# A planned opening: x split from PSUM, sums on GpSimd, and a planner that repeats its plan

## The chip, the cores and the metric

The kernel runs on one core of a Trainium2 chip. Its time is the device time of one execution in microseconds (us). TensorE is called PE here (PEld is its weight load), VectorE DVE, ScalarE ACT, GpSimd POOL and SyncE SP, as in the profile.

## The reference

One layer of a gated decoder trunk over 1024 prompt tokens and 8 sample tokens, width 1024, all in float32. What matters here:

```python
xn = _rmsnorm(h, pre_g)
proj = jnp.einsum('bld,de->ble', xn, w_in)
u, v, z_a, x_b, z_b, g_a, g_b = jnp.split(proj, SPLITS, axis=-1)
...
m = (jax.nn.sigmoid(g_a) * jnp.einsum('ble,ed->bld', y_a, w_pa)
     + jax.nn.sigmoid(g_b) * jnp.einsum('ble,ed->bld', y_b, w_pb))
h = h + _rmsnorm(jnp.einsum('bld,de->ble', m, w_out), post_g)
e = jnp.einsum('blp,pd->bld', p, w_ple)
gate = jax.nn.sigmoid(jnp.einsum('bld,de->ble', _rmsnorm(h, ple_in_g), w_pg))
h = h + _rmsnorm(gate * e, ple_out_g)
```

`y_a` and `y_b` come from two branches (a causal mix within chunks of 128 tokens, and a causal pooling), which the change does not touch. The outputs are the new h of both kinds of token and four state buffers.

## The kernel before

**Products.** Every float32 matrix is split into two parts that PE can multiply fast: `hi`, the value rounded to fp32r, and `lo`, what is left (`split`: ACT copies to hi, DVE subtracts). A product is three matmuls, hi x hi, hi x lo and lo x hi, added up in PSUM. The large products (seven column blocks of W_in, then W_pa, W_pb, W_out, W_pg) are made in 2 x 2 blocks by Strassen's scheme with seven block products, P1 to P7; the first pair of columns of v is made in the plain way with eight, as its right-hand sides are the first to be there. The right-hand sides of the scheme are four blocks of the activation (B11, B12, B21, B22: feature half, token half) and four combinations of them (T1 to T4), which `combine` makes in place in the tile `big` and `cut` splits. `product` issues the 12 matmuls of a block product, for four k, as one unit of the plan.

**The opening** (`begin`). p, W_ple, x and the first weights are loaded. 24 transposes of the identity keep PE going until data is there (`warm`). The embedding e = p W_ple is made for token tiles of 128: `p_turn` transposes and splits p, `embed` makes 2 x 6 matmuls into a PSUM region, `embed_out` copies the region to SBUF on ACT and stores it for the end of the kernel. For each x tile, ACT makes a sum of squares (`norm_root`), DVE adds epsilon, GpSimd raises to the power -0.5, and DVE scales the tile (`norm_scale`). `x_half(j, kps)` then transposes token half j of x, 8 transposes for each pair of feature blocks kp, and evacuates them with the gain from PSUM into `big`, on DVE for even kp and on ACT for odd. `xop.cut` reads `big` again to split a block: 1024 elements a partition on ACT, then on DVE. Until the end of `begin` the order of every engine is the one written there (`plan.fixed = True`).

**The planner.** Nothing is issued as it is written. `Planner.take` records each call with its duration by a formula (`duration`: for DVE 0.065 + 0.00105 us an element, plus 0.06 for scalar_tensor_tensor; for GpSimd 1.0 us for all but memset), and finds from the memory that a call touches what must come before it. Consecutive PE calls into one PSUM tile are one op, unless `apart` is called between them. `wanted` gives each op a time by which it is due (`late`), backwards from the PE ops that need it. `order` then plays the program: at each step it takes, of the ops that could start soonest, the one that is due first, and keeps a clock for each engine, for the DMA pipe and for the 46 slots of SBUF that tiles share. The order in which ops start there is the order in which the engines get their instructions; each engine works through its own in that order. PSUM is shared by 3 regions of two banks (`region`: e, pst, acc, acct) and 2 single banks (`bank`).

**The end.** The last large product is the gate h' W_pg. Its right-hand sides are pieces of W_pg (loaded as wgB and wgT, split to wgB11h, wgB11l and so on), its left-hand sides are turned tiles of the normalised h (`hn`, transposed as `pht`, split as `hw`). W_pg's pieces are loaded and split while the product before it (`acct<-woB..`) runs. h itself is put together by a DMA that adds x in flight, and then stored (`h<-h` on SP).

All instructions that pass through the planner show line 289 in the profile (`play`), so they are told apart by their tiles. [Tile names: `ph`, `pl` are the parts of p; `wehi`, `welo` of W_ple; `vw` of a weight block of v; `xB11h` and so on of x.]

Of the kernel before, what the change touches and what calls it, by code (L numbers as in the profile page):

```python
# [14 lines left out]
P = 128  # L15
D = 1024
NB = D // P
# [37 lines left out]
class Planner:  # L55
# [116 lines left out]
    def wanted(self):  # L172

        for tag, most in self.queues.items():
            live = []
            for name in [n for n in self.users if self.tags.get(n) == tag]:
                first = next(iter(self.users[name]))
                if len(live) == most:
                    over = [(max(o.seq for o in self.users[n]), n) for n in live]
                    old = min(x for x in over if x[0] < first.seq)[1]  # L180
                    first.before.update(self.users[old])
                    live.remove(old)
                live.append(name)
        for op in self.ops:
            op.waits = len(op.before)
            op.fresh = {n for n in op.names if self.tags.get(n) == "slot"}
            for o in op.before:
                o.after.append(op)
        for op in reversed(self.ops):
            took = op.busy + (op.lands + op.moved / self.RATE if op.moved else self.SEEN.get(op.engine, 0))  # L190
            ends = [o.late - took for o in op.after] + ([op.at] if op.engine == "tensor" else [])
            op.late = min(ends, default=min(op.at + 30.0, self.clock + 12.0))

    def order(self):


        self.wanted()
        free = dict.fromkeys(self.ENGINES, 0.0)
        ready = {e: [] for e in self.ENGINES}
        fixed = {e: [o for o in self.ops if o.engine == e and o.fixed][::-1] for e in self.ENGINES}  # L200
# [95 lines left out]
def hybrid_step(  # L296
# [520 lines left out]

    def x_half(j, kps):

        for kp in kps:  # L820
            ps = region("pst")
            for kk in range(2):
                k = 2 * kp + kk
                for i in range(4):
                    nc.tensor.transpose(ps[:, kk, i * P : (i + 1) * P],
                                        xts[4 * j + i][:, k * P : (k + 1) * P], ident)
# [692 lines left out]
    def p_turn(h):  # L1519
        hi, lo = pcut[h] = slot("ph", (P, 2, HALF), F32R), slot("pl", (P, 2, HALF), F32R)  # L1520
        for k in range(2):
# [4 lines left out]
            if h == 0:  # L1526
                we.cut(k)
# [20 lines left out]


    def begin():  # L1550
        psl = slot("psamp", (P, PLE))
        p_load(0)
        we.fetch(0, nc.scalar)
        for i, v in enumerate((pre_g, pool_scale, ple_in_g)):
            dma(vecs[i * NB : (i + 1) * NB, :], v[0].rearrange("(k p) -> k p", p=P), nc.scalar)
        we.fetch(1)
        for t in range(4):
            x_load(t)
        dma(xe[:NS], x_sample)
# [18 lines left out]
        norm_root(0)  # L1578
        norm_root(1)
        norm_scale(0)  # L1580
        embed(1)
        norm_root(2)
        norm_scale(1)
        norm_root(3)
        norm_scale(2)
        norm_root(S)
        norm_scale(3)
        vps = bank("vecs")
        nc.tensor.transpose(vps[:, : 3 * NB], vecs[: 3 * NB, :], ident[: 3 * NB, : 3 * NB])
        nc.vector.tensor_copy(gvec, vps[:, : 3 * NB])  # L1590
        norm_scale(S)
        embed_out(0)
        x_half(0, (0,))
        embed_out(1)
        norm_root(4)
        x_half(0, (1,))
        x_extra()
        x_half(0, (2,))
        norm_root(5)
        norm_scale(4)  # L1600
        x_half(0, (3,))
        embed(2)
        xop.cut("B11")
        norm_scale(5)
        steps[0].prepare()
        embed(3)
        xop.cut("B21")
        steps[0].run()
        norm_root(6)
        norm_root(7)  # L1610
        norm_scale(6)
        embed_out(2)
        embed_out(3)
        norm_scale(7)
# [26 lines left out]

    gvec = cpool.tile([P, 3 * NB], F32, tag="gvec", name="gvec")
    begin()
    plan.fixed = False
    for s in range(3):
        for f in steps[s].after:
            f()
# [33 lines left out]
```

## Time and profile before

| | us |
|---|---|
| median of 3 runs | 1006.89 (1005.75 to 1007.22) |
| the profiled execution | 1006.03 |
| its span, first to last instruction | 1003.7 |
| PE busy | 987.7 (98%) |
| DVE busy | 798.0 (80%) |
| ACT busy | 488.1 (49%) |
| POOL busy | 78.1 (8%) |

The granted clock of PE was 0.998 of full speed. The span is what the trace covers; 2.3 us of the execution lie around it. A row of the waits names the engine and the tile that waited, what it waited for, the us in total, how many times and the longest. A row of the order of time has the start, the duration, the engine, the line, the operation, its output and inputs, shapes and count, and in brackets the idle time before it with what ended it. An instruction's duration is longer than its pitch, since the next one of the same engine starts before it has drained.

### The profile page before, as it was taken

The numbers are of one execution on the slowest core, as the hardware profiler recorded it, in microseconds if no ns is written. First come the engines' busy times: TensorE is split into PE (matmuls) and PEld (weight loads), VectorE is DVE, ScalarE is ACT, GpSimd is POOL, SyncE is SP. The second block draws the span as 40 slices with busy tenths as digits, with TensorE's granted clock in tenths as the row PEclk, the third lists the DMA queues.
The fourth block names the chain that finished last, engine by engine and source line by source line (L and its number), as shares of the span: only waits on it lengthen the run. The fifth ranks groups of instructions, "written<-read, shape, count | busy, mean of one in ns | idle before, by whom it ended". The sixth has DMA issues, their size and how long they took to land. (4 is left out here: it accounts for less than half of the span.)

```text
span 1003.7 us, 16146 instructions
## 1 busy us (share of the span) xinstructions
PE 987.7 (98%) x6200; PEld 887.4 (88%) x6200; DVE 798.0 (80%) x1237; ACT 488.1 (49%) x887; POOL 78.1 (8%) x162
## 2 busy tenths in 40 slices
PE   8999999999999999999999999999999999998996
PEld 6889999999999999999999999999999988887885
DVE  5985448977689898887776987697799898779796
ACT  7664356555434334232433333562353365678563
POOL 2200001000000000000010100000000002312121
PEclk9999999999999999999999999999999999999999
DMA  9231213222364675441304176973764543397437
GB/s 355 115 119 43 84 43 129 85 85 86 128 234 184 233 273 197 170 169 54 120 18 146 38 249 216 313 284 122 244 222 152 181 153 84 88 305 260 128 77 219
DMA packets 85089, 160.65 MB, mean 160 GB/s; under 512 B 7422, under 2 KB 47406, under 8 KB 85005
## 3 DMA queue, kind: packets, MB, share of 16 engines
q1 hardware_dynamic: 82645, 151.72, 43.3%
q0 software_dynamic: 2048, 7.37, 4.3%
q8 instruction: 48, 0.79, 0.3%
q10 hardware_dynamic: 320, 0.54, 0.2%
q14 instruction: 28, 0.23, 0.1%
HBM read 112.49 MB, written 47.58 MB: 159 GB/s over the span
## 5 line engine op out<-in xcount | busy, mean ns | idle before, releaser
L289 DVE TENSOR_TENSOR u<-acc,u 128x520 f32<-128x520 f32 (+1 forms) x90 | 62.5, 695 | 38.7 <-PE acc L289 34.0
L289 POOL TENSOR_TENSOR rstd<-ms,mhalf 128x1 f32<-128x1 f32 (+1 forms) x45 | 41.6, 927 | 213.8 <-DVE ms L289 191.5
L289 POOL MEMSET u<- 128x8 f32 x35 | 3.5, 105 | 548.8 <-PE acc L289 268.8
L289 ACT ACTIVATE u<-acc 128x512 f32<-128x512 f32 x39 | 23.2, 595 | 36.2 <-PE acc L289 35.9
L289 ACT ACTIVATE paw<-pas 128x512 fp32r<-128x512 f32 x16 | 10.1, 629 | 30.8 <-DVE pas L289 25.5
L289 ACT ACTIVATE pbw<-pbs 128x512 fp32r<-128x512 f32 x16 | 10.0, 628 | 28.7 <-DVE pbs L289 25.5
L289 DVE TENSOR_TENSOR big<-big 128x1024 f32<-128x1024 f32 (+4 forms) x20 | 23.6, 1216 | 0.0
L289 ACT ACTIVATE zbw<-zbs 128x512 fp32r<-128x512 f32 x16 | 9.9, 628 | 27.9 <-DVE zbs L289 24.5
L289 DVE TENSOR_TENSOR xb<-acc,u 128x520 f32<-128x520 f32 (+1 forms) x12 | 8.3, 694 | 19.1 <-PE acc L289 19.1
L289 ACT ACTIVATE big<-vt 128x256 f32<-128x256 f32 x32 | 11.9, 380 | 21.4 <-PE vt L289 21.4
L289 ACT ACTIVATE big<-pht,gvec 128x128 f32<-128x128 f32 x64 | 18.0, 398 | 7.5 <-PE pht L289 7.5
L289 PE MATMUL accm<-qh,wpoolw 128*128 128x260 f32 (+1 forms) x96 | 20.9, 319 | 0.0
L289 ACT ACTIVATE big<-mix 128x256 f32<-128x256 f32 x32 | 12.1, 383 | 17.5 <-PE mix L289 16.9
L289 ACT ACT_TABLE_LOAD x13 | 16.7, 1283 | 2.9 <-PE acc L289 1.6
L289 DVE TENSOR_TENSOR v<-acc,u 128x520 f32<-128x520 f32 (+1 forms) x9 | 6.3, 697 | 14.9 <-PE acc L289 14.8
L289 DVE TENSOR_TENSOR acc<-acc,u 128x512 f32<-128x512 f32 (+1 forms) x16 | 11.1, 696 | 8.7 <-PE acc L289 8.7
L289 ACT ACTIVATE gbw<-gbs 128x512 fp32r<-128x512 f32 x16 | 10.0, 624 | 16.3 <-DVE gbs L289 14.4
L289 PEld LDWEIGHTS accm<-qh,wpoolw 128*128 128x128 f32 x96 | 15.6, 188 | 1.9
L289 DVE SCALAR_TENSOR_TENSOR zb<-accm,gvec,zb 128x512 f32<-128x512 f32 (+1 forms) x16 | 12.0, 751 | 6.6 <-PE accm L289 6.5
L289 ACT ACTIVATE xbw<-xbs 128x512 fp32r<-128x512 f32 x16 | 9.8, 624 | 14.7 <-DVE xbs L289 12.2
L289 DVE TENSOR_TENSOR big<-mix,big 128x256 f32<-128x256 f32 x32 | 13.1, 420 | 4.4 <-ACT big L289 3.5
L289 ACT ACTIVATE uw<-us 128x512 fp32r<-128x512 f32 x16 | 9.8, 627 | 13.8 <-DVE us L289 5.2
(689 smaller groups left out, 3618.3 us busy)
## 6 DMA issues: line engine op xcount, KB each, us to landing
ga<-ga SPq DMA_DIRECT2D x16, 516.0 KB
gb<-gb SPq DMA_DIRECT2D x16, 516.0 KB
ya<-za SPq DMA_DIRECT2D x8, 516.0 KB
yb<-zb SPq DMA_DIRECT2D x8, 516.0 KB
x<-in_x_prompt_dram SPq DMA_DIRECT2D x8, 512.0 KB
vraw<-in_w_in_dram SPq DMA_DIRECT2D x8, 512.0 KB
e<-e SPq DMA_DIRECT2D x8, 512.0 KB
garaw<-in_w_in_dram SPq DMA_DIRECT2D x8, 512.0 KB
```

Of the source, the lines that this page charges most:

```text
L289: getattr(getattr(self.nc, e), method)(*args, **kwargs)
```

## The change

- *Opening.* `plan.fixed` ends after the loads, so the warm-up, the embedding, the norms, x and the first products are planned like the rest. All of W_ple is loaded from SP's queue, behind the first p; before, one half went by ACT's queue. Embeddings 0 to 3 come ahead of x in program order (which also is the order in which PSUM regions are handed on), and x's halves ahead of the sample's.
- *W_ple* is split in pieces of 512 columns (`we_cut`). `embed` makes the four matmuls with W_ple's high part first, and then the two with its low part, as two units of the plan. The e copies of tiles 0 to 3 move from ACT to DVE.
- *x.* `x_half` makes hi (ACT, with the gain) and lo (DVE, scalar_tensor_tensor: PSUM times gain minus hi) straight from PSUM, 512 columns at a time. GpSimd adds hi and lo into `big`, which now serves the combinations alone. `xop.cut` of B11, B21, B12 and B22 is gone; the 8 sample columns of the second half are split from `big` as before.
- *Planner.* A GpSimd operation is priced at 0.1 + 0.0015 us an element, at least 1.0. All users of a reused buffer, not the first alone, wait for the users of the old one. `product` becomes two units, k = 0, 1 and k = 2, 3. The plan is made 40 times (`once`): after each, `hurry` looks for gaps of over 0.2 us between PE ops, goes back from the op behind the gap, up to 8 steps, each time to what ended last before it, and makes each of these due earlier. The due times that gave the earliest modelled end are used for the final plan.

```diff
@@ Planner
-    SPARED = 1.0
+    SPARED, PASSES, DEPTH = 1.0, 40, 8
...
-        return 0.1 + n * 0.0008 if method == "memset" else 1.0
+        return 0.1 + n * 0.0008 if method == "memset" else max(1.0, 0.1 + n * 0.0015)
...
-                    first.before.update(self.users[old])
+                    for user in self.users[name]:
+                        user.before.update(self.users[old])
...
     def order(self):
         self.wanted()
+        tries = []
+        for n in range(self.PASSES):
+            late = [o.late for o in self.ops]
+            self.once()
+            tries.append((max(o.end for o in self.ops), n, late))
+            self.hurry()
+        for o, o.late in zip(self.ops, min(tries)[2]):
+            pass
+        return self.once()
+
+    def hurry(self):
+        last = 0.0
+        for o in sorted((o for o in self.ops if o.engine == "tensor"), key=lambda o: o.start):
+            gap, last = o.start - last, o.end
+            for _ in range(self.DEPTH if gap > 0.2 else 0):
+                if not o.before:
+                    break
+                o = max(o.before, key=lambda b: (b.end, b.seq))
+                o.late -= min(gap, 1.0) + 0.3
@@ product
         for k in range(4):
+            if k == 2:
+                plan.apart()
@@ x_half
         for kp in kps:
-            ps = region("pst")
+            two = region("pst") if kp < 3 else None
+            ps = [bank("pst") if two is None else two[:, kk] for kk in range(2)]
...
-            out = quarter(kp, j)[:, :, :HALF]
+            hi, lo = xop.new(f"B{kp // 2 + 1}{j + 1}", kp % 2)
             for kk in range(2):
-                o, i, gain = out[:, kk], ps[:, kk], col(0, 2 * kp + kk)
-                if kp % 2:
-                    nc.scalar.activation(out=o, in_=i, func=AF.Copy, scale=gain)
-                else:
-                    nc.vector.tensor_scalar_mul(o, i, gain)
+                h, i, gain = hi[:, kk, :HALF], ps[kk], col(0, 2 * kp + kk)
+                nc.scalar.activation(out=h, in_=i, func=AF.Copy, scale=gain)
+                nc.vector.scalar_tensor_tensor(out=lo[:, kk, :HALF], in0=i, scalar=gain, in1=f32(h),
+                                               op0=ALU.mult, op1=ALU.subtract)
+            nc.gpsimd.tensor_tensor(out=quarter(kp, j)[:, :, :HALF], in0=f32(hi[:, :, :HALF]),
+                                    in1=f32(lo[:, :, :HALF]), op=ALU.add)
+            if j:
+                split(quarter(kp, j)[:, :, HALF:], hi[:, :, HALF:], lo[:, :, HALF:])
@@ we_cut, in place of we.cut(k) in p_turn
+        for k in range(2):
+            split(raw[:, k], hi[:, k], lo[:, k])
@@ embed
-            token_matmul([(ps[:, n], lambda k: hi[:, k, tok], lambda k: lo[:, k, tok])], we, n)
+            plan.apart()
+            terms = [(part[:, k, tok], we.at(n, k)[0]) for k in range(2) for part in (hi, lo)]
+            terms += [(hi[:, k, tok], we.at(n, k)[1]) for k in range(2)]
+            for i, (p, w) in enumerate(terms):
+                if i == 4:
+                    plan.apart()
+                nc.tensor.matmul(ps[:, n], p, w, start=i == 0, stop=i == 5)
@@ embed_out
-        nc.scalar.activation(out=e, in_=e_ps.pop(t), func=AF.Copy)
+        if t < 4:
+            nc.vector.tensor_copy(e, ps)
+        else:
+            nc.scalar.activation(out=e, in_=ps, func=AF.Copy)
@@ begin
-        we.fetch(0, nc.scalar)
+        we.fetch(0)
+        we.fetch(1)
...
         early_loads()
+        plan.fixed = False
...
         p_turn(0)
+        we_cut(0)
+        we_cut(1)
+        for t in range(4):
+            norm_root(t)
+            norm_scale(t)
         embed(0)
...
+        x_half(0, (0, 1))
+        steps[0].prepare()
+        x_half(0, (2, 3))
...
         steps[0].evacuate()
         x_half(1, (0, 1))
+        steps[1].run()
         p_turn(1)
         x_half(1, (2, 3))
-        steps[1].run()
-        xop.cut("B12")
         embed(4)
-        xop.cut("B22")
```

More of the change, by code (lines that the diff above doesn't have):

```diff
@@ L184, in wanted @@
         for op in self.ops:
-            op.waits = len(op.before)
-            op.fresh = {n for n in op.names if self.tags.get(n) == "slot"}
             for o in op.before:
@@ L197, in order, with once @@
         self.wanted()
+        tries = []
[16 more added lines that the diff above has]
+                o.late -= min(gap, 1.0) + 0.3
+    def once(self):
+        for o in self.ops:
+            o.waits, o.ready = len(o.before), 0.0
+            o.fresh = {n for n in o.names if self.tags.get(n) == "slot"}
         free = dict.fromkeys(self.ENGINES, 0.0)
@@ L824, in x_half @@
                 for i in range(4):
[L825 removed]
+                    nc.tensor.transpose(ps[kk][:, i * P : (i + 1) * P],
                                         xts[4 * j + i][:, k * P : (k + 1) * P], ident)
[L827 removed]
+            hi, lo = xop.new(f"B{kp // 2 + 1}{j + 1}", kp % 2)
             for kk in range(2):
[L829 to L833 removed]
+                h, i, gain = hi[:, kk, :HALF], ps[kk], col(0, 2 * kp + kk)
[6 more added lines that the diff above has]
+                split(quarter(kp, j)[:, :, HALF:], hi[:, :, HALF:], lo[:, :, HALF:])
     def x_extra():
@@ L1525, in p_turn, with we_cut @@
             split(ps, hi[:, k], lo[:, k])
-            if h == 0:
-                we.cut(k)
+    def we_cut(n):
+        raw = we.raw.pop((n, 0))
+        hi, lo = slot("wehi", (P, 2, HALF), F32R), slot("welo", (P, 2, HALF), F32R)
+        for k in range(2):
+            split(raw[:, k], hi[:, k], lo[:, k])
+        we.hi[n, 0], we.lo[n, 0] = hi, lo
     e_ps = {}
@@ L1535, in embed @@
         for n in range(2):
-            token_matmul([(ps[:, n], lambda k: hi[:, k, tok], lambda k: lo[:, k, tok])], we, n)
+            plan.apart()
[5 more added lines that the diff above has]
+                nc.tensor.matmul(ps[:, n], p, w, start=i == 0, stop=i == 5)
     def embed_out(t):
         e = slot("e", (P, 2, HALF))
-        nc.scalar.activation(out=e, in_=e_ps.pop(t), func=AF.Copy)
+        ps = e_ps.pop(t)
+        if t < 4:
+            nc.vector.tensor_copy(e, ps)
+        else:
+            nc.scalar.activation(out=e, in_=ps, func=AF.Copy)
         dma(kept["e"][t * P : (t + 1) * P].rearrange("p (n c) -> p n c", n=2), e)
@@ L1576, in begin @@
         p_turn(0)
+        we_cut(0)
[3 more added lines that the diff above has]
+            norm_scale(t)
         embed(0)
-        norm_root(0)
-        norm_root(1)
-        norm_scale(0)
+        embed_out(0)
         embed(1)
[L1582 to L1587, printed above, removed]
+        embed_out(1)
+        embed(2)
+        embed_out(2)
+        embed(3)
+        embed_out(3)
         vps = bank("vecs")
@@ L1590, in begin @@
         nc.vector.tensor_copy(gvec, vps[:, : 3 * NB])
+        x_half(0, (0, 1))
+        steps[0].prepare()
+        x_half(0, (2, 3))
+        norm_root(S)
         norm_scale(S)
[L1592 to L1596, printed above, removed]
-        x_extra()
[L1598 to L1614, printed above, removed]
+        steps[0].run()
+        x_extra()
+        for t in range(4, NB):
+            norm_root(t)
+            norm_scale(t)
         steps[1].prepare()
@@ L1643, in hybrid_step @@
     begin()
-    plan.fixed = False
     for s in range(3):
```

1 line of the change is left out of this document (removed).

## The prediction

> **What bounds the kernel now.** First the head of the page and the engines' shares, then the list of what TensorE (PE) waited for.
>
> ```profile
> span 1003.7 us, 16146 instructions
> ...
> PE 987.7 (98%) x6200; PEld 887.4 (88%) x6200; DVE 798.0 (80%) x1237; ACT 488.1 (49%) x887; POOL 78.1 (8%) x162
> ```
>
> ```profile
> PE warm L289 <- POOL ident masks.py:199: 1.9, 1, 1.9
> PE acct L289 <- DVE ms L289: 1.6, 1, 1.6
> PE acct L289 <- DVE hw L289: 1.2, 1, 1.2
> PE e L289 <- ACT wehi L289: 1.2, 1, 1.2
> PE e L289 <- DVE welo L289: 0.8, 1, 0.8
> PE pst L289 <- DVE x L289: 0.2, 1, 0.2
> PE smix L289 <- DVE sv L289: 0.2, 1, 0.2
> ```
>
> PE is busy 98% of the span and all its waits together are 7.1 us: 1.9 before the identity exists, 2.2 in the opening (e, pst), 2.8 where the last product begins (acct), 0.2 between. The change adds and removes no matmul (an embedding tile stays at 2 x 6, an x half at 32 transposes), so a gain can come only from these holes and from the stretch after the last matmul. Where the engines stand in the three places, by the view of stretches (PE, PEld, DVE, ACT, POOL busy):
>
> ```profile
> 8.84:26.38 17.54, 16.53 (x90) 13.07 (x90) 14.41 (x29) 17.11 (x28) 5.72 (x7) 1.00 1.10 386
> 26.38:64.95 38.57, 38.57 (x235) 33.79 (x233) 33.25 (x41) 25.30 (x37) 8.63 (x27) 1.00 0.29 105
> ...
> 915.50:924.10 8.60, 5.82 (x25) 4.02 (x24) 8.60 (x12) 6.80 (x12) 0.20 (x2) 1.00 0.78 208
> ...
> 994.70:1003.70 9.00, 0.02 (x1) 0.00 (x0) 4.70 (x10) 2.13 (x8) 0.59 (x1) 0.74 0.49 189
> ```
>
> In the opening ScalarE (ACT) is full (17.11 of 17.54 us), at the acct holes VectorE (DVE) is (8.60 of 8.60), and 9.00 us follow the last matmul. Elsewhere a change of order has next to nothing to gain.
>
> **Part 1, the first embedding.** The view in order of time, from the rows of PE, ACT and DVE:
>
> ```profile
> 1.93 4.72 PE L289 MATMUL warm<-ident 128*128 128x128 f32 x24 [1.93 <-POOL ident masks.py:199]
> ...
> 6.49 1.17 PE L289 MATMUL pp<-ident,p 128*128 128x128 f32 x8
> ...
> 7.25 0.60 ACT L289 ACTIVATE ph<-pp 128x512 fp32r<-128x512 f32 x1 [4.95 <-PE pp L289]
> 7.74 1.05 ACT L289 ACTIVATE wehi<-weraw 128x1024 fp32r<-128x1024 f32 x1
> ...
> 8.84 0.49 PE L289 MATMUL e<-wehi,ph 128*128 128x512 f32 x1 [1.19 <-ACT wehi L289]
> 10.11 0.50 PE L289 MATMUL e<-welo,ph 128*128 128x512 f32 x1 [0.77 <-DVE welo L289]
> 10.44 0.39 PE L289 MATMUL e<-wehi,pl 128*128 128x512 f32 x1
> 10.67 0.39 PE L289 MATMUL e<-wehi,ph 128*128 128x512 f32 x1
> ```
>
> The warm-up transposes hold PE until 6.65 whatever p does, so the turn of p stays at 6.49 (it starts as the last warm one drains). ACT's first ph starts at 7.25. Today one 1.05 us split of W_ple follows, then PE starts at 8.84. After the change the splits are 512 wide. I price one at ph's 0.60. If ACT keeps ph, ph, wehi, the third ends at 7.25 + 2 x 0.49 (the start-to-start of 7.25 and 7.74) + 0.60 = 8.83: the **first hole of 1.2 stays**. It goes only if the plan puts wehi first, which it would do if W_ple landed before p; with W_ple now behind p on SP that is unlikely. The second hole should go: four matmuls with the high part now come before the two with the low part, so the low part is asked for four matmuls after the start, 4 x 0.23 us (the pitch from 10.44 to 10.67) or at 9.8, where today it is asked for after one. I take -0.8. The pst hole of 0.2 goes as all four embeddings, not two, can fill PE before the x transposes: 48 matmuls. Low end for the part: 0; high end: all 2.2. Taken: **-1.0**.
>
> W_ple on SP costs two more 0.5 us issues ahead of x, moved from ACT's queue: x comes at most one such transfer later. PE has the embeddings to do meanwhile (48 x 0.23 = 11 us from about 9), so I cost that at nothing; without the cover it is about 1 us.
>
> **Part 2, x split straight from PSUM.** Prices from the view of groups by shape:
>
> ```profile
> L289 DVE TENSOR_TENSOR xB11l<-big,xB11h 128x1024 fp32r<-128x1024 f32 x2 | 2.4, 1222 | 1.0 <-ACT xB11h L289 1.0
> ...
> L289 DVE TENSOR_SCALAR big<-pst,gvec 128x512 f32<-128x512 f32 x8 | 5.6, 744 | 0.7 <-PE pst L289 0.6
> ```
>
> ```profile
> L289 ACT ACTIVATE big<-pst,gvec 128x512 f32<-128x512 f32 x8 | 5.1, 684 | 1.7 <-PE pst L289 1.7
> ...
> L289 ACT ACTIVATE xB11h<-big 128x1024 fp32r<-128x1024 f32 x2 | 2.0, 1056 | 0.0
> ```
>
> ```profile
> L289 DVE SCALAR_TENSOR_TENSOR zb<-accm,gvec,zb 128x512 f32<-128x512 f32 (+1 forms) x16 | 12.0, 751 | 6.6 <-PE accm L289 6.5
> ```
>
> Per group of four kp, DVE today does 4 half-wide scalings and 4 cuts: 4 x 0.744 + 4 x 1.222 = 7.9 us. After: 8 scalar_tensor_tensor from PSUM, 8 x 0.751 = 6.0. ACT: 4 x 0.684 + 4 x 1.056 = 7.0 becomes 8 x 0.684 = 5.5. For both token halves DVE gives back 3.8 us and ACT 3.0; the 16-element tails of the second half are four tiny pairs. Four of the eight e copies move from ACT to DVE; a DVE copy of 1024 from PSUM is not shown; two half-wide PSUM scalings bound it above at 1.49 and nothing below but the 0.744 of one: I take 1.4, the two-scalings price, so +5.6 on DVE. In the opening DVE had 17.54 - 14.41 = 3.1 us free, and it pays 5.6 more for copies (which must come before the third and fourth PSUM region are free for x), less what it saves. So ACT is relieved and **DVE becomes the tight engine of the opening**, within about a microsecond of holding PE. I cost it at nothing, since PE gets 24 more embedding matmuls as cover and the scaling of x tiles 4 to 7, done there today, may go later. If that cover fails, +1.
>
> **Part 3, GpSimd's eight adds.** No two-input wide operation of GpSimd is in this trace. The nearest rows are one 1024-wide select on POOL and the DVE subtraction it met:
>
> ```profile
> 63.11 1.56 POOL L289 TENSOR_SCALAR_AFFINE_SELECT ws<-ws 128x1024 f32<-128x1024 f32 x1 [25.52 <-DMA ws<-in_w_s_dram]
> ```
>
> ```profile
> 62.49 1.23 DVE L289 TENSOR_TENSOR xT3l<-big,xT3h 128x1040 fp32r<-128x1040 f32 x1
> ```
>
> ```profile
> 63.67 2.09 DVE L289 TENSOR_TENSOR xT3l<-big,xT3h 128x1040 fp32r<-128x1040 f32 x1
> ```
>
> One add: at least DVE's own price for it, 1.22; at most the select twice, 3.12; I take 1.56, the row that is nearest. Eight are 12.5 us (10 to 25) on an engine that was busy 14.4 us between 8.84 and 64.95. The two rows of DVE say more: the same subtraction took 1.23 alone and 2.09 beside the select, so GpSimd held DVE up by 0.86. The Trainium skill (GPSIMD Engine Reference, 1. Specifications) says that GpSimd shares its SBUF interfaces with VectorE and contends with VectorE instructions that have two SBUF inputs; this trace agrees, by those 0.86 us. The Trainium skill (same title, 3.1 Elementwise) gives 4497 ns for a two-input add of 2048 elements; half of that, an estimate of 2.25 us an add, would make 18 us of the eight.
>
> Who waits: the combinations T1 to T4 read the sums, and queued behind the adds on POOL are the reciprocal roots of x tiles 4 to 7.
>
> ```profile
> 43.57 6.92 DVE L289 TENSOR_TENSOR big<-big 128x1040 f32<-128x1040 f32 x6
> ```
>
> ```profile
> 69.70 0.40 PE L289 MATMUL acc<-xT2h,vw 128*128 128x260 f32 x2
> ```
>
> The first product of a combination reads xT2 at 69.70, the combinations start at 43.57, and DVE has 38.57 - 33.25 = 5.3 us free between 26.38 and 64.95 besides the 3.8 it is given. Eight holds of 0.86 (6.9 us) fit into 9.1. Cost: nothing; without that cover, 1 to 7 us, which is a rival.
>
> **Part 4, the plan repeated.** Products become two units (k below 2, and from 2), the plan is made 40 times, each time what ended last before a modelled PE gap over 0.2 us is made more urgent, and the plan with the earliest modelled end is used. This matters where the model sees the hole. At the acct holes:
>
> ```profile
> 894.61 0.15 DVE L289 TENSOR_SCALAR ms<-ssq 128x1 f32<-128x1 f32 x1 [0.84 <-ACT hn L289]
> ...
> 902.43 0.15 DVE L289 TENSOR_SCALAR ms<-ssq 128x1 f32<-128x1 f32 x1 [1.36 <-ACT hn L289]
> ...
> 919.80 0.68 DVE L289 TENSOR_TENSOR u<-acct,u 128x512 f32<-128x512 f32 x1
> 920.40 2.35 DVE L289 TENSOR_TENSOR wgB22l<-wgB,wgB22h 128x1024 fp32r<-128x1024 f32 x2
> 922.67 0.68 DVE L289 TENSOR_TENSOR hw<-hs,hw 128x512 fp32r<-128x512 f32 x1
> ```
>
> ```profile
> 893.42 0.34 SPq L289 DMA_DIRECT2D h<-h  x1
> 893.85 2.08 SPq L289 DMA_DIRECT2D wgT<-wghigh  x4
> ```
>
> DVE's pitch is 0.60 for 512 columns (919.80 to 920.40) and 1.14 for 1024 (two until 922.67). The planner's formula, 0.065 + 0.00105 n, gives 0.60 and 1.14. So its picture of this DVE-bound stretch is true and the hole lies in the plan too; haste can reach it. DVE cannot be made shorter there, but it idled 0.84 and 1.36 us shortly before, while the next pieces of W_pg were issued on SP only once h's store had gone, at 893.42. Fill those idles and the last pieces come 2.2 us sooner. Bounds: 0 (nothing moves: no room in the 46 slots) to 2.8 (both holes). Taken: **-2.2**; what is late next is hw's own low part, the last 0.6.
>
> The rest of the program was planned with 0.2 us of PE waits over 850 us and will be planned anew; 0 to +2 for a hole the model does not see. I take 0. GpSimd's new price in the planner and the wider rule for reused buffers touch only the plan and are in this. In the tail:
>
> ```profile
> 993.95 1.40 DVE L289 SCALAR_TENSOR_TENSOR ge<-ge,rstd,hback 128x512 f32<-128x512 f32 x2
> ```
>
> tile 6's last step stands before tile 7's: another order there may bring 0.6; taken 0.
>
> **Sum.** -1.0 - 2.2 = -3.2 us. The profiled execution took 1006.03 us (span 1003.7 and 2.3 around it): 1002.8, span 1000.5. The median shown, 1006.89, is 0.9 above it; against that 1003.7.
>
> **Rivals.**
> 1. *The opening gains, the acct hole stays.* The wait on SP behind h and the full DVE are both unchanged in amount, and the slots may leave no room for earlier pieces. For it: DVE is at 8.60 of 8.60. Against: 2.2 idle just before. 1006.89 - 1.0 = **1005.9**.
> 2. *GpSimd's adds hold DVE up in the opening* (slower). Each add that meets a DVE subtraction of two SBUF operands (vw, the combinations) costs 0.86, and the planner, which has no such term, cannot see it. It decides once DVE is what PE waits for before 43 us: the four adds of the first half then cost 3.4, the copies 1.0, nothing is gained in the opening. With the acct gain lost as well: 1006.89 + 4.4 = **1011.3**; with it kept 1009.1. For it: the 2.09 row. Against: the splits themselves read PSUM and only one SBUF operand, and PE has 11 us of embeddings. By the Trainium skill's figure (GPSIMD Engine Reference, 3.1 Elementwise) an estimate of a hold would be 0.86 x 2.25 / 1.56 = 1.2, and the result 1.5 us later still.
> 3. *Nothing of it is reached:* haste moves the modelled end but real holes of the same size open elsewhere. 1006.89, **within 0.2%**.
> 4. *Everything is reached:* 2.2 + 2.8 + 0.6 = 5.6: **1001.3**.
>
> **How the numbers follow.** Forecast (2 to 4.5 us gained) 0.48, rival 4 0.16, rivals 1 and 3 together 0.17, rival 2 and its milder forms 0.19. A measurement of this kernel tells about 0.2% (2.0 us) from no change, so faster is below 1004.9: 0.48 + 0.16 = 0.64; same 0.17; slower 0.19. The range leaves out the far end of rival 2 and a little beyond rival 4: 1000.8 to 1008.6.
>
> **What would show it.** Right: the e<-welo wait is gone while e<-wehi stays near 1.2; the acct waits together fall under 1; SP issues the four wgT loads well before the last hn, not after h's store; the sum of PE waits is about 3.9 with the warm one. Wrong: new PE waits on vw, on xB11l or on e copies between 15 and 45 us (part 2 or 3); DVE subtractions over 1.3 us beside POOL adds with PE waiting behind them (rival 2); acct waits of 2.8 again (rival 1); a wait on a DMA in the middle (rival 3); a stretch after the last matmul far from 9.0 us.

## The result, and the profile after

The kernel after took 1014.68 us, the median of 6 runs (1013.69 to 1016.4), where the kernel before took 1006.94 in the same job: a ratio of 1.0082 [1.0069, 1.0095]. It is slower, by 7.7 us, where 3.2 us of gain were forecast. The profiled execution took 1016.4 us (span 1014.4, before 1003.7), and 8.9 us follow its last matmul (before 9.0), so all the loss lies ahead of that. Executions of one kernel differ in their mean granted clock, and in time with it: of 55 executions of the kernel before beside the experiments, the 33 at 0.997 or 0.998 took 1005.6 us in the median, the 22 at 0.996 or less 1007.1.

The head of the page and the engines' shares of the kernel after:

```profile
span 1014.4 us, 16183 instructions
...
PE 995.3 (98%) x6200; PEld 891.5 (88%) x6200; DVE 808.6 (80%) x1247; ACT 482.2 (48%) x889; POOL 114.0 (11%) x170
```

PE has the same 6200 matmuls, but is busy 7.6 us longer. What it waited for in the kernel after (us in total, times, longest):

```profile
PE acct L313 <- DVE ge L313: 2.6, 3, 1.4
PE warm L313 <- POOL ident masks.py:199: 1.9, 1, 1.9
PE acc L313 <- DVE vw L313: 1.8, 1, 1.8
PE acc L313 <- DVE za L313: 1.0, 1, 1.0
PE vecs L313 <- DVE pl L313: 1.0, 1, 1.0
PE acc L313 <- DVE gb L313: 0.6, 1, 0.6
PE pst L313 <- DVE pl L313: 0.6, 1, 0.6
PE acc L313 <- DVE zb L313: 0.5, 1, 0.5
```

The waits add up to 10.0 us against 7.1. Both e waits are gone. New are three in the opening (vw, `vecs`, and pst behind `pl`) and three in the middle (za, gb, zb), where there were none; the acct holes are still there in other places.

Waits are only part of it. The stretch of the opening that the prediction showed, in the kernel after (busy PE, PEld, DVE, ACT, POOL, then the granted clock), and under it a closer look:

```profile
26.38:64.95 38.57, 36.14 (x205) 30.66 (x204) 34.82 (x47) 19.25 (x35) 32.65 (x20) 0.91 0.28 101
```

```profile
30.00:32.00 2.00, 1.82 (x7) 1.32 (x8) 2.00 (x6) 0.00 (x0) 2.00 (x1) 0.95 0.88 358
32.00:34.00 2.00, 2.00 (x8) 1.15 (x7) 2.00 (x4) 0.21 (x1) 2.00 (x4) 0.50 0.54 221
34.00:36.00 2.00, 2.00 (x13) 1.88 (x13) 1.92 (x4) 0.55 (x2) 2.00 (x3) 0.50 0.12 49
36.00:38.00 2.00, 2.00 (x6) 1.61 (x5) 2.00 (x1) 0.44 (x1) 1.97 (x1) 0.50 0.02 4
38.00:40.00 2.00, 2.00 (x10) 1.54 (x10) 2.00 (x7) 0.49 (x3) 0.00 (x0) 0.84 0.00 0
```

The granted clock, 1.00 all through this stretch before, is 0.91 on average and 0.50 from 32 to 38. PE counts as busy in those 6 us, yet does half the work: about 38.57 x 0.09 = 3.5 us lost, more than the wait for vw.

A second stretch at half clock comes at 164 us (0.73, 0.50 and 0.91 in three windows of 2 us, about 1.7 us lost). No wait of PE stands before it, only 16 matmuls of 8x8 from 162.11 on. Run e12 below, as fast as the kernel before, has such a stretch too (0.58 and 0.56 from 160 to 164), and what starts it was not settled. The profiled execution is also the slowest of the six: its mean clock is 0.992, that of the others 0.993 to 0.996. So its losses by the clock are larger than those of the median.

What PE waited for in the opening, and what VectorE (DVE) and GpSimd (POOL) did then, in order of time:

```profile
30.18 0.73 PE L313 MATMUL acc<-xB21h,vw 128*128 128x512 f32 x2 [1.85 <-DVE vw L313]
```

```profile
26.39 1.41 DVE L313 SCALAR_TENSOR_TENSOR xB21l<-pst,gvec,xB21h 128x512 fp32r<-128x512 f32 x2 [0.33 <-ACT xB21h L313]
27.72 2.41 DVE L313 TENSOR_TENSOR vw<-vraw,vw 128x512 fp32r<-128x512 f32 x1
30.05 1.40 DVE L313 SCALAR_TENSOR_TENSOR xB21l<-pst,gvec,xB21h 128x512 fp32r<-128x512 f32 x2
...
35.66 2.86 DVE L313 TENSOR_TENSOR vw<-vraw,vw 128x512 fp32r<-128x512 f32 x1
```

```profile
24.84 4.74 POOL L313 TENSOR_TENSOR big<-xB11h,xB11l 128x1024 f32<-128x1024 f32 x2 [1.87 <-DVE xB11l L313]
29.53 2.85 POOL L313 TENSOR_TENSOR big<-xB21h,xB21l 128x1024 f32<-128x1024 f32 x1
32.34 3.44 POOL L313 TENSOR_TENSOR rstd<-ms,mhalf 128x1 f32<-128x1 f32 x3
35.30 2.67 POOL L313 TENSOR_TENSOR big<-xB21h,xB21l 128x1024 f32<-128x1024 f32 x1
```

The subtraction of 512 elements for vw took 2.41 and 2.86 us, and 0.68 before. Read the ends: the second add of xB11 ends at 24.84 + 4.74 = 29.58, and vw at 30.13, its own 0.6 later; the add begun at 35.30 ends at 37.97, vw at 38.52. The scalar_tensor_tensor rows, which read PSUM and one SBUF operand, keep their 0.7 each beside the same adds.

### The profile page after: what moved, and what is told of

It is laid out like the page before. It is cut to its first block, busy times and chain, and to the rows that moved or that the text cites. A ratio compares the mean times of both kernels' runs of the same rounds, so it can differ in the third digit from the quotient of the medians.

```text
span 1014.4 us, 16183 instructions
## 1 busy us (share of the span) xinstructions
PE 995.3 (98%) x6200; PEld 891.5 (88%) x6200; DVE 808.6 (80%) x1247; ACT 482.2 (48%) x889; POOL 114.0 (11%) x170
## 5 line engine op out<-in xcount | busy, mean ns | idle before, releaser
L313 DVE TENSOR_TENSOR big<-big 128x1024 f32<-128x1024 f32 (+4 forms) x20 | 26.0, 1326 | 1.3 <-POOL big L313 1.3
L313 PE MATMUL acc<-xB21h,vw 128*128 128x512 f32 x40 | 14.8, 424 | 1.8 <-DVE vw L313 1.8
```

Of the source, the lines that this page charges most:

```text
L313: getattr(getattr(self.nc, e), method)(*args, **kwargs)
```

## The experiments

**Theories.** (A) GpSimd's adds: VectorE's instructions with two SBUF inputs are held while an add runs, what PE needs from them comes late, and a hole in PE is followed by half clock. (B) The new plan: products in two units, or the repetition, open holes that the model does not see. (C) The hole alone: any hole there would cost the clock, and filling it would bring the time back. Each ratio is against the kernel before, run on the same chip in the same job.

| run | median us | ratio |
|---|---|---|
| e1_fill_hole | 1015.54 | 1.0091 [1.0075, 1.0108] |
| e2_sums_on_act | 1012.74 | 1.0061 [1.0046, 1.0076] |
| e3_planner_only | 1009.35 | 1.0031 [1.0019, 1.0042] |
| e4_one_pass | 1014.94 | 1.0091 [1.0076, 1.0106] |
| e5_adds_off_gpsimd | 1009.82 | 1.0033 [1.0022, 1.0045] |
| e6_one_wide_input | 1013.33 | 1.0060 [1.0043, 1.0078] |
| e7_planner_whole_products | 1006.19 | 1.0001 [0.9991, 1.0010] |
| e8_opening_only | 1010.07 | 1.0038 [1.0023, 1.0053] |
| e9_adds_after_roots | 1011.12 | 1.0053 [1.0037, 1.0068] |
| e10_act_sums_haste | 1007.43 | 1.0018 [1.0009, 1.0026] |
| e11_act_sums_one_plan | 1010.97 | 1.0045 [1.0032, 1.0058] |
| e12_opening_adds_off_gpsimd | 1006.95 | 1.0006 [0.9997, 1.0015] |
| e13_adds_in_four | 1014.21 | 1.0078 [1.0065, 1.0091] |
| e14_opening_adds_in_four | 1011.23 | 1.0041 [1.0028, 1.0053] |
| e15_adds_in_four_haste | 1012.44 | 1.0065 [1.0051, 1.0079] |
| e16_opening_adds_in_two | 1010.48 | 1.0044 [1.0031, 1.0056] |

### Which part of the change costs: e3, e7, e4, e8

e3 is the kernel before with the new planner and products in two units; e7 the same with whole products. e4 is the change with its plan made once. e8 is the change with whole products and one plan: the new opening alone.

```diff
 # e7 and e8: one unit again for a product
         for k in range(4):
-            if k == 2:
-                plan.apart()
 # e4 and e8: one plan
-    SPARED, PASSES, DEPTH = 1.0, 40, 8
+    SPARED, PASSES, DEPTH = 1.0, 1, 8
```

> The kernel before with the planner's part of the change alone: the plan made 40 times with haste, products in two units, the wider rule for reused buffers, the new GpSimd price; the opening fixed and written as before. Theory A (the loss sits in the opening, and the planner is worth its acct gain): the opening waits stay at 2.2 us, the acct holes of 2.8 us fall under 1.5, time 1004.5 to 1006. Theory C (the repeated plan opens new holes where P3's second use of a region waits for DVE): new acc waits of 1 to 3 us between 380 and 620 us, acct holes no smaller, time 1008 to 1010.

> As the kernel before with the planner's part of the change, but products stay one unit of the plan. If the finer units are what lets the plan put P3 right behind half a product of the next pair (the holes at 396, 439 and 602 us all lie behind six matmuls of xB11): no acc wait over 0.3 us between 300 and 700 us, and 1 to 3 us less than with the units. If the haste alone does it: the same holes, the same time.

> The changed kernel with the plan made once (no haste), all else as in the change. Theory A (GpSimd's adds and the clock make the loss, whatever the plan): 1012 to 1016, with vw or x waits of 1.5 us or more before 45 us. Theory C (haste makes the loss): 1009 or less.

> The opening's part of the change alone: planned opening, x split from PSUM, adds on GpSimd, W_ple and the embedding as in the change; the plan made once and products one unit, as before. Theory A: the opening loses 5 to 6 us and the rest is as before: 1011 to 1013, no new holes between 300 and 900 us. Theory C (the loss comes from plan and units): 1006 to 1008.

The repetition with whole products costs nothing measurable (e7, 1.0001), with half products 1.0031 (e3): the **two units cost about 3 us**. The **opening alone costs about 4** (e8, 1.0038). One pass instead of 40 does not change the time of the whole change (e4 at 1.0091, the change at 1.0082, intervals overlap).

The waits of PE add up to 8.0 us in e3 and 5.3 in e7. How half products cost shows in the middle of the kernel after, PE and DVE in order of time:

```profile
395.13 0.39 PE L313 MATMUL acc<-xB11h,xbw 128*128 128x512 f32 x1
...
396.27 0.40 PE L313 MATMUL acc<-xB11h,xbw 128*128 128x512 f32 x1
397.69 0.51 PE L313 MATMUL acc<-xB22h,zaw 128*128 128x260 f32 x2 [1.02 <-DVE za L313]
```

```profile
395.55 1.27 DVE L313 SCALAR_TENSOR_TENSOR big<-big,lncol,off 128x1024 f32<-128x1024 f32 x1
396.93 1.30 DVE L313 TENSOR_TENSOR za<-acc,u 128x520 f32<-128x520 f32 x2
```

The product that begins at 397.69 needs a PSUM region that DVE is still emptying (`za`). Between the last use of that region and this product stand six matmuls, half a product, 1.4 us; DVE took a 1.27 us instruction first. Twelve matmuls, a whole product, would have covered it. The acct hole at 932 us (0.70) has the same form, half a product of wgT4 ahead of wgB22. The larger one, 1.41 us at 962.78, also stands behind six matmuls of wgT4, but there DVE came late for another reason, a store of `ge` that had not landed:

```profile
962.03 0.69 DVE L313 TENSOR_TENSOR ge<-acct,u 128x512 f32<-128x512 f32 x1 [7.24 <-DMA out_dram<-ge]
```

e3 has such a wait of DVE too (5.83 us) ahead of a hole of 1.57. In e7 the middle has no hole, and the last product has 1.4 us of waits in place of 2.8:

```profile
PE acct L313 <- DVE u L313: 0.8, 1, 0.8
PE acct L313 <- DVE hw L313: 0.4, 1, 0.4
PE acct L313 <- DVE wgT4l L313: 0.2, 1, 0.2
```

So haste does reach the acct holes, but these 1.4 us do not show in e7's median. The granted clock hides them in part: 7 of e7's ten executions had a mean of 0.995 or 0.996, against 2 of the 15 of the kernel before in the same job. The three at 0.997 or 0.998 took 1004.5 to 1004.7 us, where the kernel before took 1005.2 to 1006.7 at that clock. So haste was worth about 1 us at equal clock; whether the new order itself lowers the clock was not settled.

### What in the opening costs: e5, e12, e1

e5 keeps the order of all instructions of the kernel after, but each wide add on GpSimd becomes a copy of hi on ScalarE (the low part of x is left out of the sums). e12 is the same on the order of e8. e1 keeps the adds and puts 16 transposes of the identity in front of the matmul that waits for vw.

```diff
 # e5, e12: where the recorded calls are issued
+                if e == "gpsimd" and method == "tensor_tensor" and kwargs["out"].free_size() >= 1000:
+                    self.nc.scalar.activation(out=kwargs["out"], in_=kwargs["in0"], func=AF.Copy)
+                    continue
 # e1: in that product's op
+                        for f in range(16):
+                            late.calls.insert(2, ("transpose", (ps[:, 1, f % 4 * P : (f % 4 + 1) * P], ident, ident), {}))
```

> The changed kernel, every other engine in the same order, with each of the eight 128x1024 adds on GpSimd replaced by one ACT copy of the high part (the low part of x is left out of the sums). Theory A (an add on GpSimd holds up DVE operations of two SBUF operands: vw took 2.41 and 2.86 us instead of 0.68, and the combinations 1.74 instead of 1.15): vw is back at 0.68, PE's 1.85 us wait for it and the half clock behind it are gone, time 1014.7 - 1.9 - 3.5 = 1009.3. Theory B (the time is lost to the new order and DVE's extra e copies, GpSimd only happens to be busy then): vw stays above 2 us or PE still waits at 28 us, time above 1013.

> The opening alone (single plan, whole products), every other engine in the same order, with each GpSimd add replaced by one ACT copy of the high part (the low part of x is left out of the sums). Theory A (all of the opening's loss is GpSimd's): the waits on x, vw and xB11l go, vw 0.68 and x 0.75 us each, time 1010.1 - 4 = 1006, the same as before. Theory D (DVE's extra 5.6 us of e copies or the later x cost something too): 1007 to 1008.5, with a PE wait left between 15 and 45 us.

> The changed kernel, every engine in the same order, with 16 transposes of the identity (1.74 us at the 0.109 us pitch) put on PE just where it waited 1.85 us for DVE's vw at 28 us; they write an unused half of a PSUM region. Theory A (PE's idle hole is what lets the granted clock fall to one half from 31.6 to 38.6 us): the wait for vw stays inside the filler, PE does not idle there, the granted clock stays at full speed until 45 us and the time falls by 3.5 us of the 1014.7 to about 1011. Theory B (the clock falls for another reason, such as the load of the other engines): the clock falls at the same place all the same, and the time is 1014 to 1015.

Without the adds the change falls from 1.0082 to 1.0033 (e5), and the opening alone from 1.0038 to 1.0006, an interval that holds no difference (e12): **the opening's loss is GpSimd's adds**. In e12 DVE's rows are short again:

```profile
30.72 1.28 DVE L316 TENSOR_TENSOR vw<-vraw,vw 128x512 fp32r<-128x512 f32 x2
31.92 1.48 DVE L316 TENSOR_SCALAR x<-x,rstd 128x1024 f32<-128x1024 f32 x2
...
34.53 0.18 DVE L316 TENSOR_TENSOR xB12l<-big,xB12h 128x16 fp32r<-128x16 f32 x1
```

What is left of e5, 3.3 per mille, fits the two units (e3: 3.1, haste included).

Filling the hole (e1) did keep the clock, and brought nothing. The windows of e1:

```profile
32.00:34.00 2.00, 1.86 (x16) 1.63 (x16) 2.00 (x5) 1.00 (x2) 2.00 (x3) 1.00 0.40 164
...
36.00:38.00 2.00, 0.38 (x3) 0.02 (x1) 2.00 (x2) 0.00 (x0) 1.20 (x1) 1.00 0.00 0
38.00:40.00 2.00, 1.53 (x10) 1.53 (x11) 1.58 (x9) 0.80 (x4) 0.00 (x0) 0.78 0.00 0
40.00:42.00 2.00, 2.00 (x9) 1.82 (x8) 1.01 (x2) 1.56 (x4) 0.00 (x0) 0.50 0.01 4
```

With the hole at 28 filled and all else in the same order, the clock stays at 1.00 where it was halved: the half clock at 32 hangs on that hole (one trace of each). But now PE, ahead at full clock, reaches at 36 the x tiles that DVE has not scaled yet (2.1 us of waiting), and the half clock comes some 7 us later instead. Theory C falls: the hole is where DVE's lateness shows, and a filled hole shows it at the next place. Nor does every such hole cost the clock. In e8 PE waited 1.96 us for x, and the clock stayed at 1.00 there and in every window up to 50 us:

```profile
36.00:38.00 2.00, 0.65 (x6) 0.65 (x7) 2.00 (x6) 0.43 (x3) 0.74 (x1) 1.00 0.00 0
```

The opening's holes of 1.75 to 1.99 us in e4, e10 and e11 left it at 1.00 as well, while one of 1.34 in e16 was followed by half clock. What decides was not settled.

### Is it the hold, or GpSimd's queue: e9, e6

In e8, too, the roots of x tiles 5 to 7 stand behind adds on GpSimd's queue. e9 moves the first four adds behind the roots, everything else in e8's order. Its A2 is the hold on VectorE; the other reading is the place of the roots in the queue. e6 (order of the kernel after) adds one column of lo as a scalar, so that GpSimd reads one wide input instead of two (the rest of the low part is left out of the sums).

```diff
 # e9: in the list of calls, before it is issued
+            calls[last + 1 : last + 1] = [calls[n] for n in early]      # early: the first four adds; last: the last root
+            calls = [c for n, c in enumerate(calls) if n not in early]
 # e6: each add
-            gpsimd.tensor_tensor(out, in0=hi, in1=lo, op=ALU.add)
+            gpsimd.tensor_scalar(out, in0=hi, scalar1=lo[:, 0, :1], op0=ALU.add)
```

> The opening alone (single plan, whole products), every other engine in the same order, and on GpSimd the first four adds moved behind the reciprocal roots of x tiles 5 to 7. Theory A1 (the loss comes by GpSimd's queue: the roots wait behind adds of 2.4 to 2.8 us, so x tiles 4 to 7 are scaled late): PE's wait of 2.0 us for x falls under 0.5, time 1010.1 - 2 = 1008. Theory A2 (the loss comes by the port: DVE operations of two SBUF operands or of the fast scaling mode are held up wherever an add stands): the adds now meet the x scalings and the second half instead, x<-x still shows single operations over 1.4 us, and PE's waits before 50 us stay above 2.5 us in sum, 1009 to 1011.

> The changed kernel in the same order on every engine, with each GpSimd add reading one wide operand instead of two: the high part plus one column of the low part as a per-partition scalar (the rest of the low part is left out of the sums). Theory A: a GpSimd operation of one wide operand takes about 1.56 us and not 2.4, so the hold on vw shrinks from 1.7 to about 0.9 us; PE's wait at 28 us falls to 0.5 to 1.0 us, and if the shorter hole keeps the full clock the time is about 1010, if not about 1013. Theory B (GpSimd's length does not matter): 1014 to 1015.

e9 gained nothing: 1.0053, with the roots in time and the wait for x gone. Its rows on DVE and POOL are the clearest of all:

```profile
31.88 2.73 DVE L321 TENSOR_SCALAR x<-x,rstd 128x1024 f32<-128x1024 f32 x1
...
34.79 2.10 DVE L321 TENSOR_TENSOR xB12l<-big,xB12h 128x16 fp32r<-128x16 f32 x1
36.81 0.68 DVE L321 TENSOR_TENSOR pl<-pp,ph 128x512 fp32r<-128x512 f32 x1
37.41 1.82 DVE L321 TENSOR_TENSOR xB12l<-big,xB12h 128x16 fp32r<-128x16 f32 x1
```

```profile
31.36 5.49 POOL L321 TENSOR_TENSOR big<-xB11h,xB11l 128x1024 f32<-128x1024 f32 x2
36.81 4.72 POOL L321 TENSOR_TENSOR big<-xB21h,xB21l 128x1024 f32<-128x1024 f32 x2
```

A subtraction of **16 elements took 2.10 us**, and 0.18 in e12. That is no lower rate: it waits, and ends at 36.89 where an add ends at 31.36 + 5.49 = 36.85. `pl`, 512 elements but from PSUM and one SBUF operand, passes beside an add in 0.68. PE then waited 3.5 us for xB12l. The scaling of x is held too (2.73 against 0.74), although it reads one tensor; it is a fast one, 1024 elements in 0.74 us where a subtraction of 1040 took 1.23. The Trainium skill (GPSIMD Engine Reference, 1. Specifications) names just these two kinds, VectorE instructions with two SBUF inputs or in a mode that uses both ports, as contending with GpSimd; this trace agrees for the first, by 2.10 against 0.18, and fits the second, by 2.73 against 0.74, though no run shows which ports an instruction uses.

e6 shows another pattern. GpSimd's operation got longer (2.85 us alone, 3.67 beside DVE) and DVE's shorter (x scaled in 1.51, vw in 0.92 and 0.68): here the two seem to have taken turns within an operation. PE's waits moved from vw to x (2.0 us), since the roots come later behind the longer operations, and the time is 1.0060: a little better than the change, still slower.

### Sums elsewhere, and the adds in pieces: e2, e10, e11, e13, e14, e16, e15

e2 is the change with the sums written by ScalarE from PSUM (two ACTIVATE of 512 for each add) and no GpSimd; e10 the same with whole products; e11 as e10 with one plan. All compute the whole reference.

```diff
-            nc.gpsimd.tensor_tensor(out=quarter(kp, j)[:, :, :HALF], in0=f32(hi[:, :, :HALF]),
-                                    in1=f32(lo[:, :, :HALF]), op=ALU.add)
+            for kk in range(2):
+                nc.scalar.activation(out=quarter(kp, j)[:, kk, :HALF], in_=ps[kk], func=AF.Copy,
+                                     scale=col(0, 2 * kp + kk))
```

> The change with one part different and everything planned again: the sums are written to their tile by ACT from PSUM with the gain (16 copies of 512, 0.63 us each), not added by GpSimd. Theory A: no DVE operation of two SBUF operands over 1.3 us before 60 us, no half clock, 1008 to 1010; the 2.6 us of new PE holes at 396, 439 and 602 us and the 3 us at the acct products stay or move. Theory C (the planner's repeated haste makes the plan too tight by itself, and a new plan opens holes of the same size elsewhere): above 1011 without any GpSimd hold.

> The version that the runs so far point to: the planned opening with the sums written by ACT from PSUM, 40 plans with haste, products as one unit. If the parts add up (opening without GpSimd about 0, haste on whole products 0 to -1.2, units left out): 1004.5 to 1006.5. If a new plan opens an opening hole as in the run with the sums on ACT and products in two units (3.0 us for pl, then half clock): 1008 to 1010.

> As the run with ACT's sums, haste and whole products, but the plan made once. Theory: the acct holes are back at 2.8 us as in the kernel before and the rest is as in the plan with haste; 0.5 to 1.5 us more than that run. Rival (haste is worth nothing on the chip): the same time within 0.5 us.

With ScalarE the holds go, but PSUM banks come free later: PE waits 3.0 us in e2 and 1.3 in e10 for `pl` ahead of x's transposes, and 1.9 in e10 for the sum. e10 (1.0018) is the best of the new openings that compute everything; with one plan it is 1.0045 (e11), so here the repetition is worth some 3 us, more than the 0.5 to 1.5 expected.

The last four cut GpSimd's add into pieces as it is issued, all else in order: in four on the change (e13), in four and in two on e8 (e14, e16). e15 has whole products, 40 plans and four pieces.

```diff
+                    for kk in range(2):
+                        for c in range(0, HALF, 256):      # 512 in e16
+                            part = {k: v[:, kk, c : c + 256] if k in ("out", "in0", "in1") else v for k, v in kwargs.items()}
+                            self.nc.gpsimd.tensor_tensor(**part)
```

> Order of the kernel after; each GpSimd add of 1024 elements becomes four of 256. Hold theory (a VectorE instruction with two inputs from SBUF waits until the GpSimd add that is running has ended): no hold is longer than one piece, about 0.7 us, so vw takes at most 1.4 where it took 2.41 and 2.86, the 0.73 scalings stay, PE's wait for vw falls from 1.8 under 0.8, the half clock at 31.6 to 38.6 goes; 1010 to 1011.5. Rate theory (VectorE runs slower while GpSimd adds, whatever the size of a piece): GpSimd is busy as long or longer, vw stays at 2.4 or more, 1014 to 1017. What is left above 1007 in the first case belongs to the half products.

> New opening, one plan, whole products, in the order that gave 1010.07; each GpSimd add becomes four of 256. Hold theory: x scaled at 34.6 takes at most 1.5 instead of 2.69, PE's wait for it falls from 2.0 under 0.8; 1006.5 to 1008.5. Rate theory: 1010 to 1012, as four pieces cost GpSimd more than one.

> As the run with four pieces, but two of 512. Hold theory: holds of up to 1.3 us, a time between that with four and 1010.07: 1007.5 to 1009.5. Rate theory: 1010 to 1011, no order by the size of the piece.

> The change with whole products, its plan repeated 40 times, and GpSimd's adds in four pieces: the part of the change that is not shown to cost, put together. Hold theory: the opening costs no more than 1, haste shortens the acct holes by 1 to 1.5: 1005 to 1007.5. Rate theory: 1009 to 1011.

Times as the rate theory had them (e15, at 1012.44, above both theories), durations as the hold theory had them except in e15. The same scaling of x, in e8, e16 and e14:

```profile
34.60 2.69 DVE L313 TENSOR_SCALAR x<-x,rstd 128x1024 f32<-128x1024 f32 x1
```

```profile
35.17 1.60 DVE L319 TENSOR_SCALAR x<-x,rstd 128x1024 f32<-128x1024 f32 x1
```

```profile
36.45 1.06 DVE L319 TENSOR_SCALAR x<-x,rstd 128x1024 f32<-128x1024 f32 x1
```

The hold shrinks with the piece, 2.69, 1.60, 1.06. But it begins later each time, 34.60, 35.17, 36.45. GpSimd in e8 and in e14 says why:

```profile
29.07 2.81 POOL L313 TENSOR_TENSOR big<-xB21h,xB21l 128x1024 f32<-128x1024 f32 x1
31.85 2.72 POOL L313 TENSOR_TENSOR rstd<-ms,mhalf 128x1 f32<-128x1 f32 x3
```

```profile
30.55 3.71 POOL L317 TENSOR_TENSOR big<-xB21h,xB21l 128x256 f32<-128x256 f32 x4
34.22 2.19 POOL L319 TENSOR_TENSOR rstd<-ms,mhalf 128x1 f32<-128x1 f32 x3
```

The third add ends 2.4 us later, and the roots behind it with it. About half of that is the cutting itself: four pieces took 2.79 us undisturbed (e15, below), one add 2.39. The rest GpSimd loses beside DVE. What one engine is spared the other pays, and x waits for both. e15 adds a caution, DVE and POOL in order of time:

```profile
28.86 4.85 DVE L319 TENSOR_TENSOR vw<-vraw,vw 128x512 fp32r<-128x512 f32 x1
```

```profile
27.65 2.79 POOL L317 TENSOR_TENSOR big<-xB11h,xB11l 128x256 f32<-128x256 f32 x4
30.41 2.75 POOL L317 TENSOR_TENSOR big<-xB21h,xB21l 128x256 f32<-128x256 f32 x4
```

Here vw was held through the rest of eight pieces in a row, 4.85 us, and PE with it for 4.8: a gap between two pieces is not always DVE's turn. When it is was not settled. No version beat the kernel before.

## Why the prediction was wrong, point by point

- **What bounds the kernel: right.** The gains lay in holes of 7.1 us. That filling PE's time to 98% also makes every new hole cost was not weighed, nor was a price put on what follows a hole: 1.85 us of hole at 28 were followed by half clock from 32 to 38, about 3.5 us in the profiled execution.
- **Part 1 (-1.0): the waits roughly right, the gain not seen.** The e<-welo and pst<-x waits went as forecast, and e<-wehi, which was to stay, went too; a wait of 1.0 for `vecs` behind `pl` came in its place. The first product of e began at 9.80 where it began at 8.84, as the warm-up took longer in this execution (5.38 us, before 4.72, in e8 4.16) and `vecs` stood ahead of it. e12, which has this part, is no faster than the kernel before (1.0006).
- **Part 2 (0): sizes right.** The new splits took 0.74 against the 0.751 taken, the e copies 1.22 against 1.4. e12, where all of this is in and the adds are not, stands at 1.0006.
- **Part 3 (0): the step that failed.** Eight holds of 0.86, 6.9 us, were set against 9.1 us of DVE's free time up to 65 us. Three things in it were wrong. First the size: an add took 2.4 to 2.85 us, not 1.56 (the bound above of 3.12 holds, and the Trainium skill's figure, GPSIMD Engine Reference, 3.1 Elementwise, with its estimate of 2.25, was nearer). Second the kind: 0.86 was read as a fixed price of an encounter, while it was the rest of one 1.56 us select, which ended at 64.67, 1.0 us after the held subtraction began. The hold lasts as long as GpSimd does, so it grows with the add: 1.7 to 2.2 us for vw. Third the place: free time up to 65 us does not help vw and x, which PE wants at 28 and 36. Four adds of about 2.5 us fall between 24 and 38, where DVE had 2.4 us free in the 14 from 26 to 40 before.

  The row that counts, POOL in the kernel after:

```profile
L313 POOL TENSOR_TENSOR big<-xB21h,xB21l 128x1024 f32<-128x1024 f32 x2 | 5.5, 2762 | 0.0
...
L313 POOL TENSOR_TENSOR big<-xB12h,xB12l 128x1024 f32<-128x1024 f32 x2 | 4.7, 2392 | 5.7 <-DVE xB12l L313 5.7
```

- **Part 4 (-2.2): failed as well.** Haste was worth about half of it in the profile (acct waits 2.8 to 1.4 in e7), about 1 us at equal clock and nothing in the median. The two units were costed with "0 to +2 for a hole the model does not see" and taken as 0; they cost about 3 (e3 against e7). In the middle they do so by halving the matmuls that stand between the last use of a PSUM region and the next; at the last product the waits for ms and hw went as forecast, but new ones for `ge` took their place, the longest with a late store ahead of it.
- **The tail (0): right**, 8.9 against 9.0.
- **The rivals.** Rival 2 is what happened: its mechanism, its place (DVE is what PE waits for before 43 us) and the lost acct gain. Its price for the opening, 4.4 us, is near e8's 3.8 (a ratio of 1.0038), though of other parts: fewer and longer holds, and PE's waits for x (2.0) and vw (0.7) behind them. That nearness is partly luck. What it lacked are the two units, 3 us that no rival had, so that its 1011.3 fell 3.4 short; and the stated range ended at 1008.6, below this rival's own price. Its chance of 0.19 was too low in hindsight: the row of 2.09 us beside a select was the only evidence on the matter, and it spoke for it.
- **The sum.** 3.2 per mille for the adds (e8 less e12), 0.6 for the rest of the opening (e12; its interval holds zero) and 3.1 for units and haste (e3) make 6.9 of 8.2 per mille. Taken out of the change itself the adds are worth 4.9 (1.0082 less e5's 1.0033). The difference is inside the intervals and was not separated.

## What to carry to other kernels

Before work is given to an idle GpSimd, look at what VectorE does beside it: an instruction of VectorE with two SBUF inputs, or a fast-mode one, can wait for as long as GpSimd's own instruction lasts, so the offer is free only while VectorE reads PSUM or has nothing that is due. Where PE is at 98%, price a new hole with the half clock that can follow it, and count the matmuls that stand between the last use of a PSUM region and its next before a unit of the plan is cut in two. A cover must be free at the time at which the late thing is needed, not in the sum of a stretch.

## What the runs showed of the hardware that was not expected

- A 16-element subtraction on VectorE took 2.10 us beside a 1024-element add on GpSimd and 0.18 without it; a 512-element one 4.85 beside eight adds of 256 in a row and 0.67 without.
- The hold goes both ways: a GpSimd add of 256 took 0.73 us alone and 1.17 with VectorE's instructions between.
- GpSimd's 1024-element operation with one tensor and one column as input took 2.85 us, longer than the add of two tensors, 2.39 us.
- A hole in PE of 1.85 us, with matmuls at full clock up to it, was followed, about 1.5 us after its end, by about 7 us at half clock. A wait of 3.5 us in e9 was followed by less of it (0.91, 0.50 and 0.73 in the windows from 42 to 48), one of 1.96 in e8 by none, and at 164 us the clock fell without a wait. The Trainium skill (TensorE: Matmul & The Clock Gate, Part 1) has the clock at half or full, at half after an idle window of about 3.4 us. Half and full are what the windows show (0.50 and 1.00), but here 1.85 us of idleness sufficed.
